# Experts of a mixture layer: weights' lo parts 2048 columns at a time, and a wide expert's two tiles in one operation

## The chip, the cores and the metric

The kernel runs on one core of a Trainium2 chip. The metric is the device time of one execution in microseconds. The time before is the median of three runs.

## What is computed

The reference is one layer of a hybrid model on 1024 tokens of width 1024: a state space branch, windowed attention, a merge of both, and a mixture of 32 experts with four experts a token. The change is in the mixture alone:

```python
def expert_block(args):
    xb, e = args
    gu = xb @ w_gate_up[e] + b_gate_up[e]
    glu, lin = jnp.split(gu, 2, axis=-1)
    glu = jnp.minimum(glu, SWIGLU_LIMIT)
    lin = jnp.clip(lin, -SWIGLU_LIMIT, SWIGLU_LIMIT)
    act = glu * jax.nn.sigmoid(SWIGLU_ALPHA * glu) * (lin + 1)
    return act @ w_down[e] + b_down[e]
```

Everything is float32. The weights of an expert are 1024x2048 and 1024x1024.

## The kernel before

The core's engines are PE (matmuls), DVE and ACT (elementwise work), POOL (row gathers and scatters) and SP (issues the transfers). Each float32 operand is split in two parts for PE's faster float32r format: hi, a rounded copy that ACT writes, and lo, the rest, which DVE gets by subtracting hi from the operand. A product is then hi x hi + hi x lo + lo x hi.

The experts are ranked by how many tokens they have, and each rank has a number of slots (CAPS): 256 three times, 240, 224, 208, then 192 four times, 160 five times, and 128 seventeen times. Those over 128 are wide, the others narrow. ORDER takes them in turn, wide, narrow, wide, narrow; the last three are narrow.

An expert is twelve steps, each on 1 MB of weights. In steps 0 to 7 its gate and up products are made, in steps 8 to 11 the down product: steps 8 and 9 with the first half of the activations, steps 10 and 11 with the second. In a wide expert a step of the first kind (`up_wide`) makes two tiles of 128 features by the slots; even steps are gate, odd ones up. The tiles are read by `act_wide` in the step that follows: ACT adds the bias to one part of the sum (L1371), DVE adds the other (L1373), ACT takes the sigmoid (L1377) and DVE multiplies by it (L1380); for up, DVE clips (L1384) and multiplies by the gate (L1386), ACT writes the hi part of a (L1389) and DVE the lo part (L1394). The gate and up steps 6 and 7 make the features that the down product reads last, so PE first needs the lo part that `act_wide(7)` writes in step 10, at its third group of three matmuls.

`Weights` brings the weights. `fetch` issues 512 KB transfers on SP into `raw`, eight buffers deep. `prepare` makes hi and lo of a step (L1491 on ACT, L1493 on DVE), each for half a step at a time, into four pairs of buffers, and runs three steps ahead of PE.

The order of the operations on PE, DVE and ACT is the order in which the code issues them. In each step `weave` takes turns between the generators: the store of the expert before, `after(c)` (with `act_wide` or `act`), `prepare`, and the next expert's rows. Each goes on to its next `yield`. So the place of the yields in `act_wide` and `prepare` sets the order on ACT and DVE:

```python
weave(prev.store(1) if c == 0 and prev else None, cur.after(c), W.prepare(), x)
...
cur.main(c, W.ready.pop(0))
```

PSUM has eight banks: five for the products (K.mm), two for transposes (K.tp), and one for the slot lists (K.lg).

Of the kernel before, what the change touches and what calls it, by code (L numbers as in the profile page):

```python
# [1200 lines left out]
def slots(tc, K, pool, ps, o, info, blocks, steps=((0, 6),)):  # L1201
# [5 lines left out]
    p = ps.tile([128, 512], F32, tag="lg", name="sl")  # L1207
# [25 lines left out]
class Expert:  # L1233
# [76 lines left out]

    def up(self, c, w):

        nc, K = self.nc, self.K
        if c % 2 == 0:
            self.gu = K.mm.tile([128, 512], F32, tag="mm", name="up")
        p = self.gu
# [15 lines left out]
    def act(self, q):  # L1332
# [4 lines left out]
        t = P.tmp.tile([128, 512], F32, tag=("sg", "um")[q], name="t")[0:nb]  # L1337
# [10 lines left out]
    def up_wide(self, c, w):  # L1348
# [5 lines left out]
        self.uw = []  # L1354
        for i in range(2):
            p = K.mm.tile([128, 512], F32, tag="mm", name="uw")
# [4 lines left out]
            self.uw.append(p[:, 0:2 * n].rearrange("p (q n) -> p q n", q=2))  # L1361

    def act_wide(self, c):
# [4 lines left out]
        t = [P.tmp.tile([128, 512], F32, tag=("sg", "um")[q], name="t") for _ in range(2)]  # L1368
        x, y = [a[:, 0:n] for a in t], [a[:, 256:256 + n] for a in t]
        for i in range(2):  # L1370
            nc.scalar.activation(out=y[i], in_=self.uw[i][:, 1], func=ACTF.Identity, bias=self.bias[:, q * 8 + j0 + i:q * 8 + j0 + i + 1])  # L1371
        for i in range(2):
            v.tensor_tensor(x[i], self.uw[i][:, 0], y[i], ALU.add)  # L1373
        if q == 0:
            yield
            for i in range(2):
                nc.scalar.activation(out=y[i], in_=x[i], func=ACTF.Sigmoid, scale=SWIGLU)  # L1377
            yield
            for i in range(2):
                v.tensor_tensor(x[i], x[i], y[i], ALU.mult)  # L1380
            self.g = x
            return
        for i in range(2):
            v.tensor_scalar(x[i], x[i], LIMIT + 1, 1 - LIMIT, ALU.min, ALU.max)  # L1384
        for i in range(2):
            v.scalar_tensor_tensor(x[i], self.g[i], TOP, x[i], ALU.min, ALU.mult)  # L1386
        yield
        for i in range(2):
            nc.scalar.activation(out=self.a[:, j0 + i, 0:n], in_=x[i], func=ACTF.Copy)  # L1389
        yield  # L1390
        for i in range(2):
            hi = self.a[:, j0 + i, 0:n].bitcast(F32)
            for k, m, lo in [(0, n, 256)] if n > 192 else [(0, 128, 256), (128, n - 128, n)]:
                v.tensor_tensor(self.a[:, j0 + i, lo:lo + m], x[i][:, k:k + m], hi[:, k:k + m], ALU.subtract)  # L1394
# [27 lines left out]
    def down(self, c, k0, w):  # L1422
        if k0 == 0:
            if c == 0:
                self.y = []
            self.y.append([self.K.mm.tile([128, 512], F32, tag="mm", name="dn")[0:nb if nb > 64 else 2 * nb] for nb in self.blocks])
# [24 lines left out]
class Weights:  # L1451
# [8 lines left out]
    def add(self, eid, wide=False):  # L1460
        for m, kn, k, c in WIDE if wide else CHUNKS:
            self.todo += [(eid, m, kn // 2, k + i * kn // 2, c) for i in range(2)]

    def fetch(self):
# [5 lines left out]
        n = 1024 // kn  # L1470
# [3 lines left out]
        nc.sync.dma_start(out=r, in_=w[:, k:k + kn])  # L1474
        self.raw.append(r)

    def prepare(self):
# [6 lines left out]
        kn, n = self.raw[0].shape[1:3]  # L1484
        hi = P.ws.tile([128, 2 * kn, n], F32R, tag="wh", name="wh")
        lo = P.ws.tile([128, 2 * kn, n], F32R, tag="wl", name="wl")
        self.ready.append((hi, lo))
        for i in range(2):
# [17 lines left out]
def expert_pools(tc, a, K, es, deep):  # L1506
    P = Ctx()
    pool = lambda name, bufs=1, **k: es.enter_context(tc.tile_pool(name=name, bufs=bufs, **k))
    P.ahead = 8 if deep else 4
# [750 lines left out]
```

## Time and profile before

| | |
|---|---|
| median of 3 runs (lowest, highest) | 2746.44 us (2744.35 to 2754.49) |
| the profiled execution's own time | 2748.94 us |
| its span | 2746.8 us |
| busy, share of the span: PE, weight loads, DVE, ACT, POOL | 91%, 77%, 80%, 54%, 10% |
| mean granted TensorE clock | 0.948 |
| L1493, lo parts of the weights, DVE, 128x1024 | 768 times, 921.6 us |
| L1491, hi parts of the weights, ACT, 128x1024 | 768 times, 789.6 us |
| from the first L1493 to the last | 1099 to 2670 us |

The experts are the stage from about 1100 us to the last matmuls at about 2678 us. Before it lie the branches, attention, the merge and the routing; after it the last scatter and the closing normalisation. Shares of busy time are averages over stages with different limits, so the stage is to be read by itself. Busy PE is not PE at its peak: matmuls are pipelined, and what counts is the distance from one start to the next.

### The profile page before, as it was taken

How to read it: one execution, taken by the hardware profiler on the slowest of the kernel's cores; microseconds unless marked ns; L12 is line 12 of the kernel's file. 1: busy time of each engine (PE TensorE's matmuls, PEld its weight loads, DVE VectorE, ACT ScalarE, POOL GpSimd, SP SyncE). 2: the span in 40 equal slices, each digit the busy share in tenths (PEclk: the TensorE clock that was granted, in tenths of full speed). 3: DMA queues.
4: the chain of work that ended last, by engine and by line, in shares of the span. 5: the costliest groups of instructions: out<-in, count | busy, mean ns of one | idle time of the engine just before them, and what ended most of it. 6: DMA issues, size and time to landing. Idle time of an engine off the chain costs nothing. (4 is left out here: it accounts for less than half of the span.)

```text
span 2746.8 us, 41465 instructions
## 1 busy us (share of the span) xinstructions
PE 2513.2 (91%) x14030; PEld 2113.3 (77%) x14030; DVE 2190.4 (80%) x4354; ACT 1471.6 (54%) x2394; POOL 273.7 (10%) x173
## 2 busy tenths in 40 slices
PE   6799999889989886899999999999999999999990
PEld 1598887767778775788878878888988887888770
DVE  9735797348787757787987987988989899989995
ACT  0622112657766312555665665666666666666661
POOL 3300000000000004010100100111011011101113
PEclk8799999999999876899999999999999999999995
DMA  7434623644686782797987987998998999899984
GB/s 250 163 121 145 209 92 114 181 160 156 229 303 242 278 294 97 238 287 218 299 266 239 306 271 243 308 300 252 301 305 269 288 310 306 274 298 303 311 279 146
DMA packets 400937, 662.57 MB, mean 241 GB/s; under 512 B 36976, under 2 KB 203760, under 8 KB 393616
## 3 DMA queue, kind: packets, MB, share of 16 engines
q1 hardware_dynamic: 388416, 615.83, 67.0%
q0 software_dynamic: 11872, 42.47, 6.7%
q8 instruction: 112, 1.84, 0.3%
q10 hardware_dynamic: 432, 1.57, 0.2%
q14 instruction: 105, 0.86, 0.1%
HBM read 570.63 MB, written 89.15 MB: 240 GB/s over the span
## 5 line engine op out<-in xcount | busy, mean ns | idle before, releaser
L1493 DVE TENSOR_TENSOR wl<-raw,wh 128x1024 fp32r<-128x1024 f32 x768 | 921.6, 1220 | 162.4 <-ACT wh L1491 161.4
L1491 ACT ACTIVATE wh<-raw 128x1024 fp32r<-128x1024 f32 x768 | 789.6, 1052 | 244.0 <-PE dn L1309 88.7
L1359 PE MATMUL uw<-x,wh 128*128 128x320 f32 (+5 forms) x1920 | 578.3, 365 | 0.2 <-issue 0.2
L1360 PE MATMUL uw<-x,wl 128*128 128x192 f32 (+4 forms) x1920 | 500.2, 261 | 0.0
L1359 PEld LDWEIGHTS uw<-x,wh 128*128 128x128 f32 x1920 | 363.1, 189 | 23.5 <-issue 0.3
L1360 PEld LDWEIGHTS uw<-x,wl 128*128 128x128 f32 x1920 | 368.2, 192 | 0.5
L1306 PE MATMUL dn<-wh,a 128*128 128x512 f32 (+4 forms) x752 | 298.7, 397 | 0.0
L1307 PE MATMUL dn<-wl,a 128*128 128x512 f32 (+4 forms) x752 | 293.5, 390 | 0.0
L1309 PE MATMUL dn<-wh,a 128*128 128x512 f32 (+3 forms) x608 | 238.5, 392 | 0.6 <-DVE a L1286 0.6
L1306 PE MATMUL up<-wh,x 128*128 128x512 f32 x544 | 221.8, 408 | 0.0
L1442 POOL DMA_INDIRECT acc_d<-y,wi x47 | 118.9, 2531 | 959.5 <-DVE y L1440 815.8
L1309 PE MATMUL up<-wh,x 128*128 128x512 f32 x544 | 213.0, 392 | 0.0
L1307 PE MATMUL up<-wl,x 128*128 128x512 f32 x544 | 212.3, 390 | 0.0
L1371 ACT ACTIVATE t<-uw,bias 128x160 f32<-128x160 f32 (+5 forms) x240 | 98.6, 419 | 131.8 <-PE uw L1360 130.9
L1306 PEld LDWEIGHTS dn<-wh,a 128*128 128x128 f32 (+4 forms) x752 | 135.7, 180 | 37.8 <-issue 4.1
L1307 PEld LDWEIGHTS dn<-wl,a 128*128 128x128 f32 (+4 forms) x752 | 135.8, 181 | 33.8
L1309 PEld LDWEIGHTS dn<-wh,a 128*128 128x128 f32 (+3 forms) x608 | 112.8, 186 | 28.4 <-DVE a L1286 2.7
L1306 PEld LDWEIGHTS up<-wh,x 128*128 128x128 f32 x544 | 102.3, 188 | 27.4 <-issue 8.4
L1309 PEld LDWEIGHTS up<-wh,x 128*128 128x128 f32 x544 | 102.1, 188 | 22.4
L1307 PEld LDWEIGHTS up<-wl,x 128*128 128x128 f32 x544 | 102.4, 188 | 18.8
L51 PE MATMUL mm<-whi,uh 128*128 128x256 f32 x320 | 108.4, 339 | 4.4 <-DVE r L307 4.4
L52 PE MATMUL mm<-wlo,uh 128*128 128x256 f32 x320 | 107.7, 337 | 0.0
(529 smaller groups left out, 4970.7 us busy)
## 6 DMA issues: line engine op xcount, KB each, us to landing
raw<-w_gate_up SPq DMA_DIRECT2D x512, 512.0 KB
raw<-w_down SPq DMA_DIRECT2D x256, 512.0 KB
mw<-w_mod SPq DMA_DIRECT2D x64, 256.0 KB
raw<-w_in SPq DMA_DIRECT2D x13, 1024.0 KB
whi<-wo SPq DMA_DIRECT2D x10, 1024.0 KB
wlo<-wo SPq DMA_DIRECT2D x10, 1024.0 KB
raw<-w_mod SPq DMA_DIRECT2D x8, 1024.0 KB
gate_d<-gs SPq DMA_DIRECT2D x16, 512.0 KB
```

The costliest lines, as they stand in the source:

```text
L51: nc.tensor.matmul(out, lhsT=lsel(lh, k), rhs=rsel(rh, k), start=start and k == 0, stop=False)
L52: nc.tensor.matmul(out, lhsT=lsel(lh, k), rhs=rsel(rl, k), start=False, stop=False)
L1306: nc.tensor.matmul(ps, lhsT=h, rhs=wh[:, k], start=st, stop=False)
L1307: nc.tensor.matmul(ps, lhsT=h, rhs=wl[:, k], start=False, stop=en and nb <= 64)
L1309: nc.tensor.matmul(ps, lhsT=X[:, k0 + k, lo:lo + nb], rhs=wh[:, k], start=False, stop=en)
L1359: nc.tensor.matmul(p[:, 0:2 * n], lhsT=wh[:, k, fs], rhs=self.x[:, k, 0:2 * n], start=k == 0, stop=False)
L1360: nc.tensor.matmul(p[:, 0:m], lhsT=wl[:, k, fs], rhs=self.x[:, k, 0:m], start=False, stop=k == KT - 1)
L1371: nc.scalar.activation(out=y[i], in_=self.uw[i][:, 1], func=ACTF.Identity, bias=self.bias[:, q * 8 + j0 + i:q * 8 + j0 + i + 1])
L1442: nc.gpsimd.indirect_dma_start(out=K.acc_d, out_offset=bass.IndirectOffsetOnAxis(ap=wi[0:nb], axis=0), in_=o[0:nb], in_offset=None, bounds ...
L1491: nc.scalar.activation(out=h, in_=r, func=ACTF.Copy)
L1493: nc.vector.tensor_tensor(l, r, h, ALU.subtract)
```

## The change

- `prepare` still makes hi in two halves on ACT, but lo in one operation of 2048 columns on DVE, after both halves, in its second turn. A `raw` tile holds a whole step, filled by two transfers of 512 KB; there are four instead of eight (two instead of four in the loop for what is left over).
- K.mm has three tiles of two banks each. A wide step's two tiles lie in one of them, and `act_wide` works on both at once, except for the bias, which differs by tile. Narrow experts put two sums, or both halves of the down product, into the two banks of one tile.
- The slot lists have no bank of their own any more: they take turns with the transposes in K.tp.
- Temporaries of the activations (P.tmp) hold both tiles and have one buffer instead of two.

```diff
     def act_wide(self, c):
...
-        t = [P.tmp.tile([128, 512], F32, tag=("sg", "um")[q], name="t") for _ in range(2)]
-        x, y = [a[:, 0:n] for a in t], [a[:, 256:256 + n] for a in t]
+        t = P.tmp.tile([128, 2, 512], F32, tag=("sg", "um")[q], name="t")
+        x, y, uw = t[:, :, 0:n], t[:, :, 256:256 + n], self.uw
         for i in range(2):
-            nc.scalar.activation(out=y[i], in_=self.uw[i][:, 1], func=ACTF.Identity, bias=self.bias[:, q * 8 + j0 + i:q * 8 + j0 + i + 1])
-        for i in range(2):
-            v.tensor_tensor(x[i], self.uw[i][:, 0], y[i], ALU.add)
+            nc.scalar.activation(out=y[:, i], in_=uw[:, i, n:2 * n], func=ACTF.Identity, bias=self.bias[:, q * 8 + j0 + i:q * 8 + j0 + i + 1])
+        v.tensor_tensor(x, uw[:, :, 0:n], y, ALU.add)
         if q == 0:
             yield
-            for i in range(2):
-                nc.scalar.activation(out=y[i], in_=x[i], func=ACTF.Sigmoid, scale=SWIGLU)
+            nc.scalar.activation(out=y, in_=x, func=ACTF.Sigmoid, scale=SWIGLU)
             yield
-            for i in range(2):
-                v.tensor_tensor(x[i], x[i], y[i], ALU.mult)
+            v.tensor_tensor(x, x, y, ALU.mult)
             self.g = x
             return
...
     def fetch(self):
...
-        n = 1024 // kn
+        n = 2048 // kn
...
-        nc.sync.dma_start(out=r, in_=w[:, k:k + kn])
+        for h in range(0, kn, kn // 2):
+            nc.sync.dma_start(out=r[:, h:h + kn // 2], in_=w[:, k + h:k + h + kn // 2])
         self.raw.append(r)
...
     def prepare(self):
...
-        for i in range(2):
-            ks = slice(i * kn, (i + 1) * kn)
-            h, l, r = (x.rearrange("p k n -> p (k n)") for x in (hi[:, ks], lo[:, ks], self.raw.pop(0)))
-            nc.scalar.activation(out=h, in_=r, func=ACTF.Copy)
-            h = h.bitcast(F32)
-            nc.vector.tensor_tensor(l, r, h, ALU.subtract)
-            yield
+        h, l, r = (x.rearrange("p k n -> p (k n)") for x in (hi, lo, raw))
+        for i in (0, 1024):
+            nc.scalar.activation(out=h[:, i:i + 1024], in_=r[:, i:i + 1024], func=ACTF.Copy)
+            if i == 0:
+                yield
+        nc.vector.tensor_tensor(l, r, h.bitcast(F32), ALU.subtract)
+        yield
...
-    P.tmp = pool("etmp", 2)
+    P.tmp = pool("etmp", 1)
...
-        K.mm = pool(es, "emm", 5, space=PSUM)
+        K.mm = pool(es, "emm", 3, space=PSUM)
         K.tp = pool(es, "etp", 2, space=PSUM)
-        K.lg = pool(es, "elg", 1, space=PSUM)
```

How the change moves instructions is seen best in one gate step and one up step of a wide expert with 160 slots. In these rows uw is the pair of tiles in PSUM, t a temporary, wh and wl the hi and lo parts of the weights, a the activations; the words in brackets are the semaphores that a row waits for. On DVE, before:

```order
L1373 TENSOR_TENSOR t<-uw,t 128x160 [waits Activation_49] x2
L1493 TENSOR_TENSOR wl<-raw,wh 128x1024 [waits DMAHW5_49,Activation_49]
L1493 TENSOR_TENSOR wl<-raw,wh 128x1024 [waits DMAHW6_49,Activation_49]
L1380 TENSOR_TENSOR t<-t 128x160 [waits DVE_49] x2
L1373 TENSOR_TENSOR t<-uw,t 128x160 [waits Activation_49] x2
L1384 TENSOR_SCALAR t<-t 128x160 [waits DVE_49] x2
L1386 SCALAR_TENSOR_TENSOR t<-t 128x160 [waits DVE_49] x2
L1493 TENSOR_TENSOR wl<-raw,wh 128x1024 [waits DMAHW7_49,Activation_49]
L1493 TENSOR_TENSOR wl<-raw,wh 128x1024 [waits DMAHW0_49,Activation_49]
```

There are two subtractions between the add and the product, each of which waits for its own half from ACT. On DVE, in the changed kernel, at the same place:

```order
L1375 TENSOR_TENSOR t<-uw,t 128x2x160 [waits PE_49,Activation_49]
L1493 TENSOR_TENSOR wl<-raw,wh 128x2048 [waits DMAHW6_49,DMAHW5_49,Activation_49]
L1380 TENSOR_TENSOR t<-t 128x2x160 [waits DVE_49]
L1375 TENSOR_TENSOR t<-uw,t 128x2x160 [waits PE_49,Activation_49]
L1383 TENSOR_SCALAR t<-t 128x2x160 [waits DVE_49]
L1384 SCALAR_TENSOR_TENSOR t<-t 128x2x160 [waits DVE_49]
L1493 TENSOR_TENSOR wl<-raw,wh 128x2048 [waits DMAHW7_49,DMAHW0_49,Activation_49]
```

One subtraction stands where two stood, and it waits for both halves; the others are one operation for two. On ACT, before, at the same two steps:

```order
L1371 ACTIVATE t<-uw,bias 128x160 [waits PE_49,Activation_49] x2
L1491 ACTIVATE wh<-raw 128x1024 [waits DMAHW5_49]
L1377 ACTIVATE t<-t 128x160 [waits DVE_49] x2
L1491 ACTIVATE wh<-raw 128x1024 [waits DMAHW6_49]
L1371 ACTIVATE t<-uw,bias 128x160 [waits PE_49] x2
L1491 ACTIVATE wh<-raw 128x1024 [waits DMAHW7_49]
L1389 ACTIVATE a<-t 128x160 [waits DVE_49] x2
L1491 ACTIVATE wh<-raw 128x1024 [waits DMAHW0_49]
```

The sigmoid, or the copy into a, stands between the two weight copies and waits for DVE. On ACT, in the changed kernel:

```order
L1374 ACTIVATE t<-uw,bias 128x160 [waits PE_49,Activation_49]
L1374 ACTIVATE t<-uw,bias 128x160
L1490 ACTIVATE wh<-raw 128x1024 [waits DMAHW5_49]
L1378 ACTIVATE t<-t 128x2x160 [waits DVE_49]
L1490 ACTIVATE wh<-raw 128x1024 [waits DMAHW6_49]
L1374 ACTIVATE t<-uw,bias 128x160 [waits PE_49]
L1374 ACTIVATE t<-uw,bias 128x160
L1490 ACTIVATE wh<-raw 128x1024 [waits DMAHW7_49]
L1387 ACTIVATE a<-t 128x2x160 [waits DVE_49]
L1490 ACTIVATE wh<-raw 128x1024 [waits DMAHW0_49]
```

ACT's order is as before, with one sigmoid and one copy for both tiles.

## Rows read from the trace of the kernel before

**Rows 1.** Busy time by stage: microseconds, each engine's busy us, granted clock, DMA.

```profile
core 0: us, PE busy (x) PEld busy (x) DVE busy (x) ACT busy (x) POOL busy (x), PEclk, DMA share, GB/s
2250.00:2350.00 100.00, 99.69 (x593) 85.04 (x592) 91.55 (x184) 66.44 (x100) 11.55 (x6) 1.00 0.92 290
```

**Rows 2.** Who waited for whom, 1100 to 2670 us: total us, times, longest.

```profile
PE tp L1277 <- DVE t L1345: 4.6, 15, 0.3
...
ACT wh L1491 <- DMA raw<-w_gate_up: 0.8, 1, 0.8
```

**Rows 3.** Timeline of DVE, a wide expert of 160 slots: start, us, operation, idle before.

```profile
2237.90 1.23 DVE L1493 TENSOR_TENSOR wl<-raw,wh 128x1024 fp32r<-128x1024 f32 x1 [0.63 <-ACT wh L1491]
2239.78 1.22 DVE L1493 TENSOR_TENSOR wl<-raw,wh 128x1024 fp32r<-128x1024 f32 x1 [0.66 <-ACT wh L1491]
...
2247.78 0.55 DVE L1373 TENSOR_TENSOR t<-uw,t 128x160 f32<-128x160 f32 x2
...
2249.69 1.23 DVE L1493 TENSOR_TENSOR wl<-raw,wh 128x1024 fp32r<-128x1024 f32 x1 [0.22 <-ACT wh L1491]
...
2251.30 0.55 DVE L1373 TENSOR_TENSOR t<-uw,t 128x160 f32<-128x160 f32 x2
2251.77 0.39 DVE L1384 TENSOR_SCALAR t<-t 128x160 f32<-128x160 f32 x2
2252.07 0.56 DVE L1386 SCALAR_TENSOR_TENSOR t<-t 128x160 f32<-128x160 f32 x2
2252.54 1.22 DVE L1493 TENSOR_TENSOR wl<-raw,wh 128x1024 fp32r<-128x1024 f32 x1
...
2255.12 0.69 DVE L1394 TENSOR_TENSOR a<-t,a 128x128 fp32r<-128x128 f32 x4
2255.73 0.20 DVE L1217 TENSOR_REDUCE L<-sl 128x6 f32<-128x48 f32 x1
```

**Rows 4.** Timeline of ACT, the same two steps.

```profile
2248.14 0.57 ACT L1377 ACTIVATE t<-t 128x160 f32<-128x160 f32 x2 [1.49 <-DVE t L1373]
2248.61 1.04 ACT L1491 ACTIVATE wh<-raw 128x1024 fp32r<-128x1024 f32 x1
```

**Rows 5.** Groups of instructions: line, operation, times; busy us, mean ns; idle before.

```profile
L1341 DVE TENSOR_TENSOR t<-up,t 128x512 f32<-128x512 f32 x32 | 21.9, 684 | 0.0
L43 DVE TENSOR_TENSOR wlo<-raw,whi 128x2048 fp32r<-128x2048 f32 x22 | 50.3, 2288 | 17.2 <-ACT whi L42 17.2
```

**Rows 6.** Timeline of PE: down products begin, at 192 slots and at 160.

```profile
1788.80 0.42 PE L1306 MATMUL dn<-wh,a 128*128 128x512 f32 x1
...
2268.03 0.42 PE L1306 MATMUL dn<-wh,a 128*128 128x512 f32 x1
...
2272.44 0.39 PE L1307 MATMUL dn<-wl,a 128*64 128x512 f32 x1
```

**Rows 7.** Timeline of DVE: the last lo parts of a, same two experts.

```profile
1793.45 0.76 DVE L1394 TENSOR_TENSOR a<-t,a 128x128 fp32r<-128x128 f32 x4
...
2273.59 0.69 DVE L1394 TENSOR_TENSOR a<-t,a 128x128 fp32r<-128x128 f32 x4
```

**Rows 8.** Timeline of PE, three idle stretches before the stage; then windows behind them.

```profile
288.70 0.35 PE L51 MATMUL mm<-whi,uh 128*128 128x256 f32 x1 [2.53 <-DVE r L307]
...
501.46 0.68 PE L458 MATMUL yp<-wo,ss 128*128 128x128 f32 x4 [1.92 <-DMA wo<-wout_d]
...
1007.37 0.58 PE L53 MATMUL mm<-oh,wlo 128*128 128x256 f32 x1 [3.36 <-DMA wlo<-wa]
...
289.00:291.00 2.00, 2.00 (x13) 2.00 (x12) 2.00 (x5) 0.00 (x0) 0.00 (x0) 0.56 0.43 85
1007.40:1012.40 5.00, 5.00 (x23) 5.00 (x24) 1.21 (x4) 0.42 (x1) 0.00 (x0) 0.50 0.87 271
...
501.50:504.50 3.00, 3.00 (x25) 2.91 (x26) 0.25 (x1) 0.26 (x1) 0.00 (x0) 1.00 0.79 247
```

**Rows 9.** Timelines of DVE and PE, a late narrow expert: product, then transposes.

```profile
2655.72 0.69 DVE L1345 SCALAR_TENSOR_TENSOR t<-t 128x512 f32<-128x512 f32 x1
...
2657.12 0.38 PE L1277 MATMUL tp<-ident,t 128*128 128x128 f32 x2
```

More of the change, by code (lines that the diff above doesn't have):

```diff
@@ L1309, in product, with banks @@
                 nc.tensor.matmul(ps, lhsT=X[:, k0 + k, lo:lo + nb], rhs=wh[:, k], start=False, stop=en)
+    def banks(self, name):
+        return self.K.mm.tile([128, 2, 512], F32, tag="mm", name=name)
     def up(self, c, w):
         nc, K = self.nc, self.K
-        if c % 2 == 0:
-            self.gu = K.mm.tile([128, 512], F32, tag="mm", name="up")
-        p = self.gu
+        if c % 4 == 0:
+            self.both = self.banks("up")
+        p = self.gu = self.both[:, c // 2 % 2]
         self.product(0, p, self.x, c % 2 * 4, w, c % 2 == 0, False)
@@ L1353, in up_wide @@
         wh, wl = w
-        self.uw = []
+        t = self.banks("uw")
         for i in range(2):
-            p = K.mm.tile([128, 512], F32, tag="mm", name="uw")
+            p = t[:, i]
             fs = slice(i * 128, (i + 1) * 128)
@@ L1425, in down @@
                 self.y = []
-            self.y.append([self.K.mm.tile([128, 512], F32, tag="mm", name="dn")[0:nb if nb > 64 else 2 * nb] for nb in self.blocks])
+            if self.wide or c == 0:
+                self.dn = self.banks("dn")
+            self.y.append([self.dn[0:nb if nb > 64 else 2 * nb, b if self.wide else c] for b, nb in enumerate(self.blocks)])
         for b in range(len(self.blocks)):
@@ L1461, in add @@
         for m, kn, k, c in WIDE if wide else CHUNKS:
-            self.todo += [(eid, m, kn // 2, k + i * kn // 2, c) for i in range(2)]
+            self.todo.append((eid, m, kn, k, c))
     def fetch(self):
@@ L1508, in expert_pools @@
     pool = lambda name, bufs=1, **k: es.enter_context(tc.tile_pool(name=name, bufs=bufs, **k))
-    P.ahead = 8 if deep else 4
+    P.ahead = 4 if deep else 2
     P.raw = pool("eraw", P.ahead)
@@ L1629, in lists @@
                     r = ORDER[i]
-                    return slots(tc, K, P.li, K.lg, o, lambda t: K.info[:, t, r, :], BLOCKS[CAPS[r]], *steps)
+                    return slots(tc, K, P.li, K.tp, o, lambda t: K.info[:, t, r, :], BLOCKS[CAPS[r]], *steps)
             def start(i, ls):
@@ L1638, in start @@
                 return e
-            P.ahead = 2
+            P.ahead = 1
             with tc.manual_schedule(engines={mybir.EngineType.PE, mybir.EngineType.DVE, mybir.EngineType.Activation}):
@@ L1648, in moe @@
                 regs.clear()
-                P.ahead = 8
+                P.ahead = 4
                 for x in cur.x_parts():
@@ L1752, in rest @@
             W.add(eid)
-            e = Expert(tc, K, P, (128,), pk, next(slots(tc, K, P.li, K.lg, places(tc, K, P.li, lambda t: pos[:, t:t + 1], 128),
+            e = Expert(tc, K, P, (128,), pk, next(slots(tc, K, P.li, K.tp, places(tc, K, P.li, lambda t: pos[:, t:t + 1], 128),
                                                         lambda t: inf[:, t, :], (128,))))
```

31 lines of the change are left out of this document (14 added, 17 removed).

## Prediction

> **What bounds the kernel now.** I read the table of stages first. From about 1150 to 2650 us, the experts, PE is busy 99.7% of a hundred microseconds at a granted clock of 1.00, and DVE 91.6% [rows 1]. Then the list of waits: past its first microseconds PE waits 4.6 us in all there, on one line, and ACT waits 0.8 us for a weight transfer [rows 2]. So PE sets the pace, the transfers are in time, and a faster DVE can by itself give back hardly anything. What can move the time is a chain between ACT and DVE that runs late enough to stop PE. I therefore read the DVE and ACT timelines of one pair of steps of a wide expert of 160 slots [rows 3, 4], and then where that chain stands against PE at the point where PE needs its last product [rows 6, 7].
>
> The pair is to be read like this. DVE adds (2247.78), subtracts one half of the weights, waits 0.22 us for ACT, subtracts the other half, multiplies, adds again, and so on. It reaches the same point of its list at 2255.73, so a pair takes it 7.95 us, with hardly a gap. The two subtractions of a step are its filler: the first one runs while ACT does the sigmoid and the second copy of the weights.
>
> **The lo parts 2048 columns at a time (the main term).** The order of the change puts ACT's sigmoid (or its copy into a) in front of the second weight copy, and DVE's one subtraction needs both copies. So between DVE's add and its subtraction nothing is left to do on DVE. The idle time there is 0.04 us hand-over, the sigmoid of both tiles, 0.10 us less because the next ACT operation starts that much before the listed end (2248.14 + 0.57 against 2248.61), the copy of 1.04 us, and 0.04 us hand-over (2248.61 + 1.04 against 2249.69) [rows 3, 4]. The sigmoid is two operations and 0.57 us now; as one it is not above that, I take 0.47. The sum is 1.49 us, against 0.22 us now.
>
> A pair of steps on DVE after the change, with one operation on 320 elements at 0.48 us (two of 160 take 0.55 us [rows 3], one of 512 takes 0.684 us [rows 5]), the subtraction of 2048 at 2.29 us [rows 5], and 0.09 us of overlap between neighbours (2252.07 + 0.56 against 2252.54):
>
> - gate step: add 0.48 + idle 1.49 + subtraction 2.29 + product 0.48 - 0.18 = 4.56 us;
> - up step: add 0.48, clip 0.33, product 0.48, where each of the last two now needs the result of the operation just ahead and so gains no overlap but 0.03 us of gap = 1.35; idle 1.49; subtraction 2.29; lo parts of a 0.60; less 0.18 = 5.55 us.
>
> Together 10.1 us, about 2.2 us more than 7.95. The bounds are 1.5 us (if every merged operation costs a third less than I take) and 2.9 us (if merged operations gain nothing at all and hand-overs double).
>
> What the rows show is thus a pair whose gaps the halves fill, 0.22 us idle at each. "Perfetto Trace Analysis" of the Trainium skill, Optimizing Scalar/DVE Operations, says that grouping into larger operations can improve throughput if the engine is saturated, and, two paragraphs on, that where these engines are not saturated but cause bubbles on others, breaking instructions up may let work finish sooner. By the first rule this term would be a gain of at most the 4.6 us that PE waits; by the second a loss, as the rows have it.
>
> There are four pairs in a wide expert. In the first, DVE already waits 0.63 and 0.66 us for ACT [rows 3] rather than twice 0.22, so 0.85 us of it is not new: 1.35 us. The chain ends 1.35 + 3 x 2.2 = about 8.0 us later. At 192 slots the idle time and the subtraction are the same and the merged operations a little longer on either side, so I take 8.0 there too.
>
> **What that meets on PE.** The last operation of the chain writes the lo parts of a. PE needs them in the down product's third step, at its ninth matmul. Down matmuls follow each other by 0.23 us (nineteen from 2268.03 to 2272.44) [rows 6]; the first two steps hold 40 at 160 and 192 slots, so the need comes 48 x 0.23 = 11.0 us after the down product starts: 2268.03 + 11.0 = 2279.1 at 160 slots, 1799.8 at 192. The lo parts are done at 2273.59 + 0.69 = 2274.28 and 1793.45 + 0.76 = 1794.21 [rows 7]. The cover is 4.8 and 5.6 us. A delay of 8.0 leaves PE standing 3.2 us in each of the five experts of 160 slots and 2.4 us in each of the four of 192: 16.0 + 9.6 = 25.6 us. At 208 slots the second block takes twelve matmuls a step instead of eight, which puts the need 8 x 0.23 = 1.8 us later: cover 7.4, stall 0.6 us. Wider ones have more cover. Term: **+26 us**. The ready weights, prepared three steps ahead, do not help: it is the activations that are late, not the weights.
>
> **The clock behind each stall.** After PE stood idle for 2.53 us the granted clock was 0.56 of full over the next two microseconds, after 3.36 us it was 0.50 for five; after 1.92 us it stayed at 1.00 [rows 8]. 0.50 is the 1.2 GHz level, where the same matmuls take twice as long. The stalls of 3.2 us lie among the first two, those of 2.4 just below them. Three to six microseconds at the lower level lose half of themselves, 1.5 to 3 us; I take 1.8 for each of nine: **+16 us**. Bounds: nothing, and 27 us.
>
> **Pairs of PSUM banks.** Three pairs instead of five single banks: a wide step's pair comes back after three steps, before after two and a half. The down product's second step needs the pair of the seventh step of gate/up, whose add is some 6 us late by then; PE may wait there 0.1 to 0.6 us, but the later stall ends at the same moment, so this adds nothing. The slot lists now take one of the two transpose banks, in the sixth step. The next transposes take turns with it; nearest row, 0.3 us [rows 2]. I take 0, bound +5 us over 32 experts.
>
> **Narrow experts.** There the transposes of the activations wait for the clip and product on DVE, which now stand behind an operation of 2.29 us instead of 1.22, up to 1.07 us later. At 2655.72 the product ends 0.71 us before PE wants it [rows 9]. So 0 to 0.36 us at each of 34 places; DVE is behind ACT in these experts, when a merged subtraction ends no later than two, and I take 0, bound +12 us.
>
> **The rest.** One tile of 1 MB is refilled after its one subtraction, where its first half came free a step's half earlier. ACT waits 0.8 us on a weight transfer in the whole stage [rows 2], so I take 0; if that cover were gone it would show first in the last three experts, by a few microseconds. The issue order on SP differs only in where the expert numbers are loaded, in front of transfers that are steps ahead: 0. At the start of the stage, PE's first weights come after a 2.29 us operation instead of the second 1.22: +1 us. Temporaries with one buffer are written again two steps after their last reader: 0. What DVE saves in operations is inside the 10.1 us.
>
> **Sum.** 26 + 16 + 1 = +43 us on the profiled execution's 2748.9 us, 2792 us. The median of the runs is 2.5 us below that execution, so I forecast **2789 us**. About 0.5%, 14 us, is what a measurement of this kernel can tell from no change.
>
> **Rivals.**
>
> - The stalls without the clock: they last 2.4 to 3.2 us, near the shortest idle time that the rows show followed by the lower level. 2746 + 27 = 2773 us. For it: 1.92 us did not lower it. Chance 0.20.
> - The cover holds, so no slower. The point from which it decides is an extra of 1.4 us a pair (4 x 1.4 - 0.85 = 4.75): the place is the same wait of PE for the lo parts. It needs a merged operation and hand-over much cheaper than the two singles show. 2747 us. Chance 0.11.
> - DVE's relief counts: with fewer operations DVE runs ahead, and what PE still waits for it goes. That is 4.6 us [rows 2]: 2741 us. For it: DVE is at 91.6% [rows 1]. Against it: the idle time on DVE is part of the chain, and fewer operations don't shorten it. Chance 0.04. (This is how the grouping rule above would have it.)
> - More than forecast: an extra of 2.9 us a pair puts the delay at 10.8 us, stalls of 6.0, 5.2 and 3.4 us at 160, 192 and 208 slots, 54 us, and 2.5 us of clock at ten places: 2746 + 54 + 25 + 1 = 2826 us. Chance 0.07.
>
> **How the numbers follow.** The forecast has 0.58. The range leaves out the two cases that are no slower (0.15) and the top of the last (0.05): 2758 to 2825 us. Faster by over 0.5% (below 2733) is beyond even the third rival: 0.02. Within 0.5% are the second and third: 0.13. Slower: 0.85.
>
> **What would show it.** Right: in wide experts of 160 and 192 slots, PE waits of 2 to 4 us for the lo parts of a, nine or ten of them, in the third step of the down product; DVE idle about 1.5 us before each subtraction, released by ACT's weight copy; a pair of steps near 10.1 us on DVE; granted clock below 1.00 in windows behind the stalls; DVE's busy share lower while the stage is longer; experts of 256 slots as long as before. Wrong: no such PE waits, with the lo parts done before the ninth matmul; or PE waits on another release, such as weights (wl) or PSUM pairs.

## The result, and where the time went

| | median, us | lowest to highest, runs |
|---|---|---|
| before | 2748.0 | 2744.35 to 2754.49, 4 |
| after | 2989.8 | 2985.45 to 2993.82, 4 |

The ratio is 1.0877, 95% interval [1.0862, 1.0893]: 242 us slower, where 41 to 43 were forecast. The direction was right, and the time lies 165 us above the range.

The table of stages of the changed kernel (from, to, length, PE's busy time, granted clock, share of the transfers, GB/s), for the experts' stage, for a hundred microseconds like those of [rows 1], and for some pieces that are used below:

```profile
1132.19:2921.40 1789.21, 1638.01 (x8462) 0.95 0.76 244
2300.00:2400.00 100.00, 89.56 (x470) 0.95 0.81 261
2457.00:2460.00 3.00, 0.00 (x0) 1.00 0.99 301
2460.00:2462.00 2.00, 1.85 (x7) 0.86 1.07 358
2462.00:2465.00 3.00, 3.00 (x8) 0.52 1.03 309
2465.00:2468.00 3.00, 3.00 (x13) 1.00 0.89 292
```

The same stage of the kernel before, with the same 8462 matmuls:

```profile
1123.00:2678.58 1555.58, 1550.08 (x8462) 1.00 0.89 281
```

So of the 242 us between the two spans (2988.4 and 2746.8), 146 are PE standing still (1789.2 - 1638.0 = 151.2, before 5.5), 88 are PE busy for longer with the same matmuls, and 9 lie ahead of the stage; behind it 1 comes back. The second share is the clock: behind a stop it falls to the 1.2 GHz level (0.52 of full from 2462 to 2465). Within five microseconds it does so behind 44 of the stage's 57 stops of over 1.3 us.

Who PE waits for in the changed kernel (total us, times, longest); [rows 2] had 4.6 us here:

```profile
PE up L1306 <- DVE t L1344: 83.1, 34, 4.8
PE dn L1306 <- DVE y L1438: 39.5, 17, 3.0
PE dn L1309 <- DVE a L1390: 23.6, 11, 2.9
...
PE dn L1306 <- DVE t L1375: 3.7, 5, 1.2
```

The third line is the forecast's stall, 23.6 us where 26 were expected. The first two are waits that the forecast does not have: they lie in the 17 narrow experts, two in each expert's gate/up sums and one in its down sums. One of them on PE's timeline:

```profile
2456.32 0.49 PE L1323 MATMUL up<-bgu,pk 64*128 64x512 f32 x1
2460.15 0.50 PE L1306 MATMUL up<-wh,x 128*128 128x512 f32 x1 [3.34 <-DVE t L1344]
...
2461.79 0.63 PE L1306 MATMUL up<-wh,x 128*128 128x512 f32 x1
...
2465.29 0.40 PE L1306 MATMUL up<-wh,x 128*128 128x512 f32 x1
```

At 2456.81 the gate sum is done, in the first bank of a pair. The up sum goes into the second bank. It starts only when DVE's product (line 1344), which reads the first bank, has ended at 2460.09. And DVE, whose timeline of this piece and of a pair of wide steps just ahead of it follows, gets to that product late:

```profile
2420.71 0.47 DVE L1375 TENSOR_TENSOR t<-uw,t 128x320 f32<-128x320 f32 x1
2422.67 2.29 DVE L1493 TENSOR_TENSOR wl<-raw,wh 128x2048 fp32r<-128x2048 f32 x1 [1.48 <-ACT wh L1490]
...
2430.35 0.69 DVE L1286 TENSOR_TENSOR x<-tp,x 128x512 fp32r<-128x512 f32 x1
...
2431.41 0.48 DVE L1375 TENSOR_TENSOR t<-uw,t 128x320 f32<-128x320 f32 x1
...
2456.62 2.27 DVE L1493 TENSOR_TENSOR wl<-raw,wh 128x2048 fp32r<-128x2048 f32 x1
2458.82 0.67 DVE L1286 TENSOR_TENSOR x<-tp,x 128x512 fp32r<-128x512 f32 x1
2459.42 0.67 DVE L1344 TENSOR_TENSOR t<-up,t 128x512 f32<-128x512 f32 x1
```

The product stands behind a subtraction of 2.27 us and a put of x (the lo part of the next expert's transposed rows), though ACT's sigmoid was done at 2457.44. In a narrow expert of the kernel before the product ends as late, 3.44 us behind the gate sum (2202.72 against 2199.28). It costs nothing there: each sum has a bank of its own, and PE goes on at once. PE's timeline, then DVE's:

```profile
2198.79 0.49 PE L1320 MATMUL up<-bgu,pk 64*128 64x512 f32 x1
2199.22 0.50 PE L1306 MATMUL up<-wh,x 128*128 128x512 f32 x1
```

```profile
2202.04 0.68 DVE L1341 TENSOR_TENSOR t<-up,t 128x512 f32<-128x512 f32 x1
```

### The profile page after: what moved, and what is told of

Read it like the earlier page. It is cut to its first block, busy times and chain, and to the rows that moved or that the text cites. A ratio compares the mean times of both kernels' runs of the same rounds, so it can differ in the third digit from the quotient of the medians.

```text
span 2988.4 us, 40046 instructions
## 1 busy us (share of the span) xinstructions
PE 2600.1 (87%) x14030; PEld 2164.9 (72%) x14030; DVE 2155.2 (72%) x3574; ACT 1448.9 (48%) x2274; POOL 236.5 (8%) x173
## 5 line engine op out<-in xcount | busy, mean ns | idle before, releaser
L1493 DVE TENSOR_TENSOR wl<-raw,wh 128x2048 fp32r<-128x2048 f32 x384 | 878.0, 2290 | 384.5 <-ACT wh L1490 382.6
L1362 PEld LDWEIGHTS uw<-x,wh 128*128 128x128 f32 x1920 | 364.3, 190 | 23.5
L1306 PE MATMUL dn<-wh,a 128*128 128x512 f32 (+4 forms) x752 | 316.2, 421 | 43.2 <-DVE y L1438 39.5
L1306 PE MATMUL up<-wh,x 128*128 128x512 f32 x544 | 240.5, 442 | 83.1 <-DVE t L1344 83.1
L1307 PE MATMUL dn<-wl,a 128*128 128x512 f32 (+4 forms) x752 | 307.6, 409 | 0.0
L1309 PE MATMUL dn<-wh,a 128*128 128x512 f32 (+3 forms) x608 | 249.6, 410 | 23.6 <-DVE a L1390 23.6
L1307 PE MATMUL up<-wl,x 128*128 128x512 f32 x544 | 229.4, 422 | 0.0
L1309 PE MATMUL up<-wh,x 128*128 128x512 f32 x544 | 228.9, 421 | 0.0
L1306 PEld LDWEIGHTS up<-wh,x 128*128 128x128 f32 x544 | 113.0, 208 | 118.9 <-DVE t L1344 91.7
L1440 POOL DMA_INDIRECT acc_d<-y,wi x47 | 72.6, 1544 | 1017.0 <-DVE y L1438 892.7
L1309 PEld LDWEIGHTS up<-wh,x 128*128 128x128 f32 x544 | 112.4, 207 | 26.4
L1307 PEld LDWEIGHTS up<-wl,x 128*128 128x128 f32 x544 | 113.0, 208 | 22.4
L1255 POOL DMA_INDIRECT x<-xm_d,ri x47 | 61.7, 1312 | 681.6 <-DVE L L1217 373.7
```

Of the source, the lines that this page charges most:

```text
L1255: nc.gpsimd.indirect_dma_start(out=x[0:nb], out_offset=None, in_=K.xm_d, bounds_check=S - 1, oob_is_err=True, in_offset=bass.IndirectOffse ...
L1306: nc.tensor.matmul(ps, lhsT=h, rhs=wh[:, k], start=st, stop=False)
L1307: nc.tensor.matmul(ps, lhsT=h, rhs=wl[:, k], start=False, stop=en and nb <= 64)
L1309: nc.tensor.matmul(ps, lhsT=X[:, k0 + k, lo:lo + nb], rhs=wh[:, k], start=False, stop=en)
L1362: nc.tensor.matmul(p[:, 0:2 * n], lhsT=wh[:, k, fs], rhs=self.x[:, k, 0:2 * n], start=k == 0, stop=False)
L1440: nc.gpsimd.indirect_dma_start(out=K.acc_d, out_offset=bass.IndirectOffsetOnAxis(ap=wi[0:nb], axis=0), in_=o[0:nb], in_offset=None, bounds ...
```

## Experiments

Theory A, made from these rows, is that a write into one bank of a pair waits for the readers of the other. Its rival B is that three pairs are too few. The table gives, for every kernel that was run, the median, its ratio to the kernel before, and, for its own experts' stage, PE's idle time (before 5.5 us) and its busy time above the 1550.1 us of before. The stage begins in every kernel 2.1 us after PE's last long wait for an expert's rows has ended, and ends with the last down matmul, which makes 8462 matmuls in each.

| kernel | us | ratio [95%] | PE idle | busy, more |
|---|---|---|---|---|
| after | 2989.8 | 1.0877 [1.0862, 1.0893] | 151 | +88 |
| 1a own_tiles | 2814.5 | 1.0247 [1.0230, 1.0264] | 46 | +18 |
| 1b own_up | 2868.4 | 1.0437 [1.0407, 1.0466] | 84 | +37 |
| 2a split_lo | 3030.0 | 1.1024 [1.1006, 1.1043] | 181 | +107 |
| 2b split_late | 2838.6 | 1.0325 [1.0308, 1.0342] | 77 | +17 |
| 3a lo_alone | 2782.1 | 1.0124 [1.0107, 1.0141] | 32 | +7 |
| 3b lo_first | 2754.2 | 1.0016 [1.0004, 1.0028] | 10 | -2 |
| 4a own_split | 2779.8 | 1.0122 [1.0105, 1.0139] | 24 | 0 |
| 4b own_all | 2758.0 | 1.0035 [1.0022, 1.0049] | 14 | -1 |
| 4c copy_first | 2777.2 | 1.0113 [1.0093, 1.0133] | 25 | +8 |
| 4d swap | 2754.0 | 1.0008 [0.9995, 1.0021] | 7 | +1 |
| 5 lists_tp | 2750.2 | 1.0002 [0.9990, 1.0015] | 7 | +2 |
| 6a repaired | 2758.4 | 1.0030 [1.0017, 1.0044] | 12 | +1 |
| 6b repaired2 | 2766.0 | 1.0069 [1.0051, 1.0086] | 17 | -1 |
| 6c repaired3 | 2769.8 | 1.0088 [1.0063, 1.0113] | 22 | +2 |

### 1. No shared pair in narrow experts

own_tiles gives each sum of a narrow expert a pair of its own; own_up does so for gate/up alone.

```diff
     def up(self, c, w):
-        if c % 4 == 0:
+        if c % 2 == 0:
             self.both = self.banks("up")
-        p = self.gu = self.both[:, c // 2 % 2]
+        p = self.gu = self.both[:, 0]
...
     def down(self, c, k0, w):
-            if self.wide or c == 0:
-                self.dn = self.banks("dn")
-            self.y.append([self.dn[0:nb if nb > 64 else 2 * nb, b if self.wide else c] for b, nb in enumerate(self.blocks)])
+            self.dn = self.banks("dn")
+            self.y.append([self.dn[0:nb if nb > 64 else 2 * nb, b] for b, nb in enumerate(self.blocks)])
```

> The changed kernel, but in narrow experts no two sums share a pair of banks: each gate/up sum and each down sum takes a pair of its own and uses its first bank. Theory A (shared pair): PE's first matmul into the second bank of a pair waits until the readers of the first bank are through, though the banks differ. Then PE's waits in the up products on DVE's product (83.1 us, 34 times) and in the down products on DVE's store (39.5 us, 17 times) go, and with them the half clock behind them; the waits of the down products on DVE's a-lo (23.6 us, 11 times) stay, and the time is what the forecast chain alone costs: 2775 to 2805 us. Theory B (too few buffers): three pairs turn over faster than five single banks did and PE waits for the oldest. Then using only half of each pair makes it no better: 2950 us or more, with the same waits under other tiles.

> The changed kernel with pairs of their own for the narrow experts' gate/up sums alone; their two down sums still share a pair. Theory A (a write into one bank of a pair waits for the readers of the other): the waits of the up products on DVE's product (83.1 us) go, the waits of the down products on DVE's store (39.5 us, 17 times) stay at 30 to 45 us. Both edits together gave 2814.5 us; the down's waits and the half clock behind 17 of them put back some 39.5 + 17 x 1.8 = 70 us at most: 2860 to 2885 us. Rival D (the two waits are one delay that runs through the expert, and PE catches up elsewhere): the down's waits shrink with the up's, under 15 us, and the time is under 2835 us.

PE's waits in own_tiles, then in own_up:

```profile
PE dn L1309 <- DVE a L1390: 21.9, 11, 2.9
PE tp L1277 <- DVE t L1348: 20.3, 19, 2.7
...
PE dn L1306 <- DVE t L1375: 3.7, 5, 1.2
```

```profile
PE dn L1306 <- DVE y L1438: 39.5, 17, 3.0
PE dn L1309 <- DVE a L1390: 25.1, 11, 2.9
```

In own_tiles both waits are gone and 175 us come back, with half of each pair empty: three pairs are enough, and B falls. The time is 10 us over what was expected. The second row shows why: the transposes now wait 20.3 us for DVE's later product (line 1348); behind the earlier stops of the changed kernel it was 1.3 us. In own_up the time is in its range and the down's waits are 39.5 us to the tenth, so the two do not run into each other (D falls). So 122.6 us of the idle time are shared pairs of narrow experts.

### 2. The subtraction cut in two, pairs kept

split_lo puts a subtraction behind each half of the copy, one in each turn, which is the order of the kernel before; split_late puts both into the second turn.

```diff
         for i in (0, 1024):
-            nc.scalar.activation(out=h[:, i:i + 1024], in_=r[:, i:i + 1024], func=ACTF.Copy)
-            if i == 0:
-                yield
-        nc.vector.tensor_tensor(l, r, h.bitcast(F32), ALU.subtract)
-        yield
+            s = slice(i, i + 1024)
+            nc.scalar.activation(out=h[:, s], in_=r[:, s], func=ACTF.Copy)
+            nc.vector.tensor_tensor(l[:, s], r[:, s], h[:, s].bitcast(F32), ALU.subtract)
+            yield
```

> The changed kernel with the weights' lo part again in two subtractions of 1024 columns, each behind its own half of ACT's copy; pairs of banks as in the change. Theory A (shared pair): the waits stay in number (34 and 17), but DVE reaches the product sooner, since a subtraction of 1.2 us and not one of 2.3 us stands ahead of it: some 1 us less each, 51 waits, 50 us with the clock's share at 0.6 us per us of wait, 80 us; the a-lo waits (23.6 us) go too: 2870 to 2920 us. Theory C (the long subtraction is the whole cause, the pairs none of it): back to 2748 us, within 10.

split_lo was a miss: 40 us slower than the change, not 70 to 120 faster. DVE's timeline of split_lo at one wait, PE's sum having ended at 2477.40, and then PE's row:

```profile
2478.10 2.34 DVE L1492 TENSOR_TENSOR wl<-raw,wh 128x1024 fp32r<-128x1024 f32 x2
2480.37 0.67 DVE L1286 TENSOR_TENSOR x<-tp,x 128x512 fp32r<-128x512 f32 x1
2480.97 1.20 DVE L1492 TENSOR_TENSOR wl<-raw,wh 128x1024 fp32r<-128x1024 f32 x1
2482.11 0.67 DVE L1344 TENSOR_TENSOR t<-up,t 128x512 f32<-128x512 f32 x1
```

```profile
2482.92 0.77 PE L1306 MATMUL up<-wh,x 128*128 128x512 f32 x1 [5.52 <-DVE t L1344]
```

One more subtraction, at 2480.97, stands ahead of the product. It belongs to the same turn as the sigmoid. So with the kernel before's own order of subtractions, the rest of the change alone costs 282 us (3030.0 against 2748.2), and beside the shared pairs the long subtraction saves 40 us. Theory C falls: the pairs do not need the long subtraction to cost what they cost. The row gave theory H.

```diff
         for i in (0, 1024):
             s = slice(i, i + 1024)
             nc.scalar.activation(out=h[:, s], in_=r[:, s], func=ACTF.Copy)
+            if i == 0:
+                yield
+        for i in (0, 1024):
+            s = slice(i, i + 1024)
             nc.vector.tensor_tensor(l[:, s], r[:, s], h[:, s].bitcast(F32), ALU.subtract)
-            yield
+        yield
```

> The changed kernel with its subtraction cut in two of 1024 columns that both stay where the change has the one, in the weave's second turn, behind the narrow expert's product (the first split put one of them in the first turn, ahead of the product, and gave 3030 us instead of 2990). Theory H (DVE's product, for which PE waits at a shared pair, comes late by what stands ahead of it in DVE's queue: in the first split that is a subtraction which waits for a copy that ACT makes behind the sigmoid): without it the time is again that of the change, 2975 to 3000 us, with 75 to 95 us of waits in the up products. Rival I (two short subtractions are worse of themselves, by their number): 3015 us or more.

PE's waits in split_late, and the table of stages (the busy times of PE, weight loads, DVE, ACT, POOL; clock) behind one of 2.67 us that ended at 2455.05, and behind another of 2.67 us that ended at 2256.57:

```profile
PE up L1306 <- DVE t L1344: 54.2, 34, 2.8
PE dn L1306 <- DVE y L1438: 22.9, 17, 2.0
```

```profile
2455.00:2457.00 2.00, 1.95 (x9) 1.62 (x10) 2.00 (x2) 0.00 (x0) 2.00 (x1) 1.00 1.00 350
2256.57:2258.57 2.00, 2.00 (x5) 1.61 (x6) 2.00 (x2) 0.00 (x0) 2.00 (x1) 0.50 0.99 323
```

The subtraction's place matters, as H says, and rival I falls, but the size was missed by some 140 us: 2838.6, well under the change. Against the change, the same 51 waits are 45 us shorter (77.1 for 122.6), the waits for the lo parts of a, 23.6 us, are gone, and PE's busy time is 71 us less, because the clock falls behind 7 of its 26 stops of over 1.3 us, not behind 44 of 57. The two windows show that the length of a stop does not settle it alone. That the first half can be subtracted while ACT still makes the second would be why DVE comes 0.6 to 1 us sooner. The trace has such a place (ACT's two copies from 2447.79 to 2449.91, DVE's subtractions from 2448.52), but as the cause it is argued from the order; no run has it alone.

### 3. The 2048 columns alone

lo_alone is the kernel before with the change's `fetch` and `prepare` only. lo_first moves one `yield` in it:

```diff
         for i in (0, 1024):
             nc.scalar.activation(out=h[:, i:i + 1024], in_=r[:, i:i + 1024], func=ACTF.Copy)
-            if i == 0:
-                yield
+        yield
         nc.vector.tensor_tensor(l, r, h.bitcast(F32), ALU.subtract)
         yield
```

> The kernel before with one part of the change alone: raw weights and the lo part 2048 columns at a time; single PSUM banks, two operations for two tiles. The forecast chain (ACT's sigmoid ahead of the second half of the copy, DVE's one subtraction behind it): stalls of PE's down products on DVE's a-lo of 20 to 30 us in about eleven waits and the half clock behind them: 2775 to 2800 us. If the long subtraction alone costs what the change does: 2980 us. If it costs nothing without the pairs: 2748 us, within 8.

> The kernel before with the lo part 2048 columns at a time (2782.1 us in that form), but with both halves of ACT's copy in the weave's first turn, ahead of the sigmoid; DVE's subtraction stays in the second turn. The forecast's chain (the sigmoid stands ahead of the second half of the copy, and DVE's subtraction waits for it): the waits on DVE's a-lo (8.3 us), on its sums at line 1373 (9.4 us) and most of those of the transposes (13.8 us) go: 2748 to 2760 us. Rival G (the long subtraction itself, 2.3 us at the head of DVE's queue, makes the steps late, whatever ACT does): it stays at 2775 to 2790 us.

PE's waits in lo_alone:

```profile
PE tp L1277 <- DVE t L1345: 13.8, 18, 1.2
...
PE dn L1309 <- DVE a L1394: 8.3, 9, 1.1
...
PE dn L1306 <- DVE t L1373: 6.0, 8, 1.0
```

lo_alone costs 34 us, as the chain says, though the stop is spread: with five single banks PE already waits at the sums (6.0 us here, 3.4 us more at the first products), and 8.3 us are left at the lo parts of a. lo_first, with the same long subtraction, costs 5 us: G falls. The price was the sigmoid ahead of the second copy, not the grouping. "Perfetto Trace Analysis" of the Trainium skill, Optimizing Scalar/DVE Operations, has one rule for grouping (a saturated engine) and one against (bubbles on others); these two kernels are grouped alike and differ by 28 us, so here neither rule decides, but what the grouped operation waits for does.

### 4. The wide experts' shared pair

own_split has the edits of own_tiles and split_lo; own_all besides this puts the two blocks of a wide expert's last down sum into pairs of their own.

```diff
-            self.dn = self.banks("dn")
-            self.y.append([self.dn[0:nb if nb > 64 else 2 * nb, b] for b, nb in enumerate(self.blocks)])
+            t = [self.banks("dn") for _ in self.blocks[:c + 1]]
+            self.y.append([t[b * c][0:nb if nb > 64 else 2 * nb, b] for b, nb in enumerate(self.blocks)])
```

> Both edits: pairs of their own in narrow experts, and the lo part in two subtractions of 1024 columns. What is left of the change is the wide experts' pair of banks with one operation for both tiles, the slot lists' bank and the single temporary. If theory A and the forecast chain are all there is: 2748 us, within 10. Above 2765 us a third cause is at work (the wide pair's reuse, the temporaries); below 2738 the merged operations bring something.

> Pairs of their own in narrow experts and the lo part in two subtractions (2779.8 us), and besides this the two sums of a wide expert's last down products in pairs of their own, each in one bank. Theory E (the mirror of A: DVE's store of the first block waits until PE has written the second block into the other bank of the pair, some 1.9 us, and DVE is late by as much in the narrow expert behind it, where PE's transposes wait for it): the transposes' waits on DVE's product at line 1348 fall from 23.6 us to 4 to 8 us, and the time to 2752 to 2764 us; what is left over 2748 is the start, where the slot lists' bank takes a transposes' bank (PE waits some 4 us more there). Rival F (the single temporary of each kind, or the merged operations, make DVE late): the waits stay at 20 us or more and the time at 2780 us.

own_split is 32 us over the kernel before, so there is a third cause. PE waits 23.6 us (before 4.6) in the transposes of the narrow experts, each of which comes behind a wide one; in own_all it waits 13.5. The two rows:

```profile
PE tp L1277 <- DVE t L1348: 23.6, 15, 2.4
PE tp L1277 <- DVE t L1348: 13.5, 15, 1.3
```

F falls, and the time of own_all is in E's range, but half of the waits go, not the three quarters that E gave. DVE's timeline of own_split, and then ACT's, at the store of a wide expert (a block of at most 64 slots has its sum in two parts, of which `whole` has ACT copy one and DVE add the other):

```profile
2202.82 0.75 DVE L1437 SCALAR_TENSOR_TENSOR y<-dn,gt,g 128x512 f32<-128x512 f32 x1
2204.29 0.68 DVE L1332 TENSOR_TENSOR hg<-dn,hg 32x512 f32<-32x512 f32 x1 [0.72 <-ACT hg L1331]
```

```profile
2203.67 0.59 ACT L1331 ACTIVATE hg<-dn 32x512 f32<-32x512 f32 x1 [2.02 <-DVE y L1437]
```

No writer of the pair is involved. ACT's copy reads the second block's bank, DVE's store reads the first block's, and the copy waits 2.02 us until the store is through. Before, it was the other way round, ACT's copy and then DVE's store:

```profile
2189.28 0.59 ACT L1328 ACTIVATE hg<-dn 32x512 f32<-32x512 f32 x1
```

```profile
2190.43 0.74 DVE L1440 SCALAR_TENSOR_TENSOR y<-dn,gt,g 128x512 f32<-128x512 f32 x1
```

That is theory J, that readers of one pair stand in line too. It also explains the half: own_all parts the blocks in the second of an expert's two down sums only, and DVE's sum (line 1332) waits for ACT's copy 18 times in own_split, 12.9 us, and nine times in own_all, 6.5 us. The first attempt at it, copy_first, issued ACT's copy at the head of the store:

```diff
+        copies = [self.copied(self.y[c][b], nb) for b, nb in enumerate(self.blocks)]
         for b, nb in enumerate(self.blocks):
-            y = self.whole(self.y[c][b], nb, "hg")
+            y = self.summed(self.y[c][b], nb, copies[b])
             yield
```

(`copied` and `summed` are the two operations of `whole`.)

> The kernel with pairs of their own in narrow experts and two subtractions (2779.8 us; both blocks of a wide expert's down sum in one pair), with one edit: a wide expert's store issues ACT's copy of the second block's half ahead of DVE's read of the first block, not behind it. Theory J (two readers of one tile stand in line too: ACT's copy from one bank waits until DVE has read the other, as 2203.67 behind 2202.82 + 0.75 in that kernel; twice an expert, about 1 us each): DVE is no longer late in the narrow expert behind it, the transposes' waits at the product fall from 23.6 us to 4 to 9 us, and the time to 2752 to 2762 us, though both blocks still share a pair. Theory E as first put (DVE's store of the first block waits until PE has written the second): the waits stay at 18 us or more and the time over 2772 us.

It gave 2777 us and 24.5 us of waits, which was the sign set down against J, but it decides nothing: the edit also put the copy ahead of ACT's weight copies, where it stands for 2.8 to 3.5 us and holds them up. swap changes only which reader is issued first:

```diff
         for b, nb in enumerate(self.blocks):
-            y = self.whole(self.y[c][b], nb, "hg")
+            y = self.summed(self.y[c][b], nb, t)
             yield
...
+            if b + 1 < len(self.blocks):
+                t = self.copied(self.y[c][b + 1], self.blocks[b + 1])
             nc.vector.scalar_tensor_tensor(o[0:nb, cs], y[0:nb], gt[0:nb], K.g2[0:nb, cs], ALU.mult, ALU.mult)
```

> The kernel with pairs of their own in narrow experts and two subtractions (2779.8 us), with one edit: in a wide expert's store ACT's copy of the second block is issued just ahead of DVE's read of the first block, in the same turn. Neither engine's own order changes (ACT: weight half, copy, weight half; DVE: subtraction, first block, sum, subtraction, second block); only which of the two readers of the pair has to stand behind the other. Theory J (readers of one tile stand in line, whatever banks they read): ACT's copy no longer waits 2 us for DVE, DVE's sum has no idle time in front of it, the transposes' waits at the product fall from 23.6 us to 5 to 12 us, and the time to 2755 to 2768 us. Against it: waits of 18 us or more and 2772 us or more.

ACT's timeline of swap, then DVE's, then PE's wait:

```profile
2194.50 0.59 ACT L1340 ACTIVATE hg<-dn 32x512 f32<-32x512 f32 x1
```

```profile
2195.65 0.75 DVE L1455 SCALAR_TENSOR_TENSOR y<-dn,gt,g 128x512 f32<-128x512 f32 x1
2196.32 0.67 DVE L1347 TENSOR_TENSOR hg<-dn,hg 32x512 f32<-32x512 f32 x1
```

```profile
PE tp L1277 <- DVE t L1363: 4.8, 12, 0.5
```

The copy runs before the store, DVE's sum follows without a gap, and the time is that of the kernel before, at the lower end of what J gave or just under it. J stands. swap also keeps the merged operations, the single temporaries and the lists in a transposes' bank: none of them costs anything that shows.

### 5. The slot lists

lists_tp is the kernel before with this, and `K.tp` for `K.lg` in the two calls of `slots`:

```diff
-    p = ps.tile([128, 512], F32, tag="lg", name="sl")
+    p = ps.tile([128, 512], F32, tag="tp", name="sl")
```

> The kernel before with one part of the change alone: the slot lists' sums in the transposes' two banks. If that is what makes the start longer: PE's waits in the first experts' transposes (8.2 us on the loads and 7.6 us on DVE in the kernel before) are 4 to 5 us longer together, and the time is 2751 to 2754 us. If the start's waits come from the larger raw loads or from the pairs: no more than 1 us.

Nothing: 1.0002. The start's waits are only divided otherwise. The 9 us at the start of the changed kernel are not this alone; with lo_alone PE's two long waits there are already 2.6 us longer (9.0 and 8.6 us, before 7.6 and 7.3). From the first slot lists to the first expert product the changed kernel takes 23.5 us, the kernel before 18.4, lists_tp 17.8 and lo_alone 19.9, so neither part has it by itself, and the rest was not taken apart.

### 6. The change, mended

To the changed kernel, repaired applies the edits of own_tiles, lo_first and own_all; repaired2 those of own_tiles, lo_first and copy_first; repaired3 those of own_tiles, lo_first and swap.

> The changed kernel with all that the theories name mended: no pair shared by sums that are read at different times (narrow experts' up and down, a wide expert's last down products), and both halves of ACT's copy ahead of the sigmoid. Kept: the lo part in one subtraction of 2048 columns, one operation for both tiles of a wide step, the slot lists in a transposes' bank, one temporary of each kind. If shared pairs and the order of ACT's copies are the whole cost: 2750 to 2765 us, with DVE's busy time some 40 us under the kernel before. If the 2048 columns or the merged operations cost something of themselves: over 2775 us. Faster than before by 0.5% would be under 2734 us, which no theory expects, since PE is busy for nearly all of this stage.

> The changed kernel with three things mended: pairs of their own in narrow experts, both halves of ACT's copy ahead of the sigmoid, and ACT's copy of a wide store's second block ahead of DVE's read of the first; the wide experts keep both blocks in one pair. If these three are the whole cost but for the start: 2750 to 2760 us, with PE's waits at the transposes' product at 4 to 9 us, where the mend that took further pairs instead gave 2758.4 us and 11.8 us. If the pair of a wide expert's down sums costs more than the order of its two readers: over 2768 us. No theory expects it under 2740 us: DVE's busy time falls by some 40 us, but PE waits for little of it.

> The changed kernel with pairs of their own in narrow experts, both halves of ACT's copy ahead of the sigmoid, and the two readers of a wide store swapped as in the run beside it. Theory J: 2750 to 2760 us, at or under the 2758.4 us of the mend that gave the wide experts further pairs. Against it: 2765 us or more, as the mend that moved the copy ahead of the weights (2766.0 us).

In repaired the time is in its range. DVE is busy 2148.6 us, 42 less than before, and the time is 10 us more, not less. The other two, with an order of the readers in place of further pairs, lose 8 and 11 us by it. repaired2 was expected at 2750 to 2760 us or over 2768 and came out between. repaired3 was expected at 2750 to 2760 and is at 2769.8, the sign set down against J. But its DVE timeline shows J's line of readers with the roles exchanged:

```profile
2197.51 0.75 DVE L1455 SCALAR_TENSOR_TENSOR y<-dn,gt,g 128x512 f32<-128x512 f32 x1 [2.70 <-ACT hg L1340]
```

ACT's copy now stands behind both early weight copies, and DVE's store, issued after it, waits 2.70 us for it. No version beats the kernel before; swap equals it.

## Why the prediction was wrong, point by point

- **What bounds the kernel.** Right. PE does, and what DVE saves gives nothing back: repaired shows it with 42 us. (The list of waits has 0.6 us more than the one line read from it, in two waits of the last experts.)
- **The main term, the chain in the wide experts.** Right in mechanism and size. The idle time was forecast at 1.49 us and is 1.48 to 1.49. The pair of steps was forecast at 10.1 us; it is 10.70 from 2420.71 to 2431.41, of which 0.60 is a put of x that takes its place there; the next pair, to 2441.54, has none and takes 10.13. Stalls: 23.6 us for 26, in eleven waits: 2.88 us at each 160-slot expert for 3.2, and 1.2 to 2.9 at 192 slots for 2.4. Alone (lo_alone) it costs 34 us, for 43 with its clock, though only 8.3 us of waits lie where the forecast has them.
- **The clock behind each stall.** The sum of it was about right where there are only about as many stops as forecast, by some luck; the number of stops was wrong. own_tiles has ten stops of over 1.3 us, six of them the forecast's, and PE is busy 18 us longer, for 16 forecast; but a lower clock follows six of the ten, at some 3 us each, not all ten at 1.8. That 1.92 us is too short, as the forecast took from one row, does not hold (last section). In the changed kernel it is 88 us, since there are 51 further stops at the pairs.
- **"Pairs of PSUM banks … I take 0, bound +5" and "Narrow experts … I take 0, bound +12".** These are the steps that failed. The wait that the first one does name is there (0.63 us four times, 1.19 once, at the down product's second step). But I asked how soon a pair comes round again, and in the narrow experts only for the transposes. I did not ask which two sums lie in one pair and when each is read and written: 122.6 us of waits, where own_tiles gets back 175 us with the clock's share. The diff had it: `self.both[:, c // 2 % 2]`, one tile for the gate and the up sum, and the gate's product is issued just ahead of the up's first matmul.
- **Parts that were summed.** Their costs don't add. The long subtraction alone costs 34 us (lo_alone), the rest of the change alone 282 (split_lo), both together 242. With single banks, or pairs of their own (own_tiles against own_split, 35 us), the long subtraction costs what the chain says; with shared pairs it saves 40 us, since one subtraction fewer stands ahead of the narrow expert's product. With both subtractions behind that product (split_late) the change as a whole costs 89. DVE's lateness, which single banks forgive, is handed to PE at each shared pair.
- **Readers of a wide pair.** Not seen. Some 25 us (own_split against swap), hidden in the changed kernel behind earlier stops.
- **Slot lists and temporaries at 0.** Right. **Start +1**: it was 9, of which 2 lie ahead of the first slot lists (1089.19 against 1087.23).
- **Rivals.** Stalls without the clock, the cover that holds and DVE's relief are all refuted; "more than forecast" had the side and not the cause.

## What to carry to other kernels

Before two PSUM sums are put into one tile, write down for each who reads it and when the other is written: a tile of two banks was one thing here, for writers and for readers, and PE's next sum waited for the last one's reader. Price a grouped operation by the latest of what it waits for and by what stands behind it in its queue; one moved `yield` was worth 28 us. Where two parts of a change make the same engine late and make others wait for it, their costs don't add (34 and 282 us alone, 242 together): look for the new wait first, and only then at how late its releaser is.

## What the runs showed that I had not expected

- The clock falls behind stops that are shorter than the 1.92 us after which it had stayed at 1.00 [rows 8]. PE's row and the window behind it in the changed kernel:

```profile
1218.30 0.50 PE L1306 MATMUL up<-wh,x 128*128 128x512 f32 x1 [1.79 <-DVE t L1344]
```

```profile
1218.30:1220.30 2.00, 2.00 (x6) 0.68 0.84 265
```

It did not fall behind three waits of 2.67 us in split_late, and did behind two others of 2.67 us. Longer stops are followed by it more often (all ten of over 3 us in the changed kernel, 14 of the 22 of under 2.1 us), but no length divides them. The fall can come after PE has gone back to work: the matmuls of 2460.15 and just behind it still take 0.50 and 0.40 us, that of 2461.79 takes 0.63, and that of 2465.29 takes 0.40 again; behind the stop that ended at 1239.54 the clock is at 0.50 from the start. What else decides it, no run here takes apart.
- The waits at the pairs are semaphore waits that the kernel's program carries. In the kernel before DVE reads one bank (2202.04 to 2202.72) while PE writes another. Whether the two banks of one pair would themselves have let a reader and a writer go side by side, no run here shows.
